# First phase of a two-layer diffusion backbone: quarter loads, modulation two chunks ahead, a fixed TensorE order, and later loads held back

## Chip, core and metric

The kernel runs on one core of a Trainium2 chip. The time is the device time of one execution in microseconds (us); the figure compared is the median of several executions. The kernel before took 1450.68 us (three runs, 1450.13 to 1450.79).

## What is computed

The reference runs two layers over 256 latent tokens and 256 context tokens of width 1024. Only the head of the first layer matters here:

```python
c_act = jax.nn.silu(c)
cc_act = jax.nn.silu(c_ctx)
...
mod = (c_act @ w_mod[i] + b_mod[i]).reshape(b, N_MOD, 1, d)
modc = (cc_act @ w_mod[i] + b_mod[i]).reshape(N_MOD, 1, d)
h = rms_norm(x, norm1_g[i]) * (1 + mod[:, 1]) + mod[:, 0]
hc = rms_norm(xc, norm1_g[i]) * (1 + modc[1]) + modc[0]
p = split_cols(h @ w_in[i])
pc = split_cols(hc @ w_in[i])
```

Six modulation vectors come from `w_mod`; the first two (scale and shift) must exist before the normalised input `h` can be formed, and `h` is needed by every projection in `w_in`. Four attention branches, a gated merge and a gated feed-forward network follow, then the second layer.

## The kernel before

**Tiling.** Everything is held transposed: the width 1024 is `KD` = 8 chunks of 128 partitions, the 512 tokens (256 latent, then 256 context) are the columns. Products are made in three parts: an operand is split into a rounded high half and the rest (`wh` and `wl` for weights, `hh` and `hl` for the input), and `mm3` (before, lines 278 to 280) multiplies high by high, high by low, low by high.

**The first phase.** It ends when the neighbourhood branch's keys and values (called keys below) are done. Its parts are:

- `xt`, the input, arrives in two loads; ScalarE squares its eight chunks, VectorE adds them into `ssf`. `rstd` (line 403 and on) sums over partitions on TensorE, takes the power -1/2 on GpSimd and spreads the result over partitions with TensorE again.
- `mods_chunk(c)`, for each chunk c: two 512-KB tiles of `w_mod` are loaded (`mraw`, line 370), sixteen products on TensorE give the scale and shift of chunk c (line 372), ScalarE copies them out of PSUM (`t`, line 375), two transposes turn them (line 378), VectorE reduces four parts into `M` (line 380).
- `modulate`: VectorE makes `t` from input, scale `s1` and `rstd`; ScalarE adds the shift and rounds, giving `hh` (line 424); VectorE forms the rest `hl`. This is done twice a chunk, for latent and for context tokens.
- `kv_mm`: twelve products of 512 columns a chunk, into three `acc` buffers and one `av` buffer of PSUM. The weights are four 512-KB tiles `raw` (line 264), two chunks each; ScalarE rounds a tile to `wh` (line 272), VectorE makes `wl` (line 257). Four buffers each exist for `raw`, `wh` and `wl`, and the next stages' weights use the same ones.

After the phase ScalarE copies values (`Vt`) and keys (`st`) out of PSUM, which frees an `acc` buffer for the query block `naq` (weights: two more tiles). The copy `dgt` (line 990) and the rope tables `rt` on GpSimd (line 257) need two 256-KB loads (lines 988 and 992). Between the attention stages `mods` computes the later modulation vectors on VectorE (`junk`, line 350, from a `raw` tile and `cact`, the activated conditioning spread over partitions).

**What sets the order.** Each engine runs its instructions in the order in which the build lists them. The build takes that order from a planner, which models when each instruction could start; the order in the source is only its input. All loads are issued by SyncE, one after the other, with eight in flight at most: a load waits until the eighth before it has landed, and for its buffer.

The names above and the lines that the change touches are in these functions:

## Time and profile before

| | |
|---|---|
| median of three runs | 1450.68 us |
| profiled execution | 1446.25 us, of which 1444.1 us span |
| TensorE busy | 1401.8 us (97% of the span) |
| VectorE, ScalarE, GpSimd busy | 1047.4, 657.8, 203.5 us |
| chain that ended last | TensorE 91%, VectorE 3%, ScalarE 2% |
| granted TensorE clock, mean | 0.994 of full speed |
| load traffic | 199.69 MB read, 139 GB/s over the span |

TensorE is busy nearly all the time, so a share of the whole span says little: what can move is where TensorE stands still, and most of that lies in the first 61 us. The views to read are the busy time by stretch for that part, and the timeline, whose bracket tells how long an engine stood before an instruction and what ended the wait.

### The profile page before, as it was taken

The numbers are of one execution on the slowest core, as the hardware profiler recorded it, in microseconds if no ns is written. First come the engines' busy times: TensorE is split into PE (matmuls) and PEld (weight loads), VectorE is DVE, ScalarE is ACT, GpSimd is POOL, SyncE is SP. The second block draws the span as 40 slices with busy tenths as digits, with TensorE's granted clock in tenths as the row PEclk, the third lists the DMA queues.
The fourth block names the chain that finished last, engine by engine and source line by source line (L and its number), as shares of the span: only waits on it lengthen the run. The fifth ranks groups of instructions, "written<-read, shape, count | busy, mean of one in ns | idle before, by whom it ended". The sixth has DMA issues, their size and how long they took to land.

```text
span 1444.1 us, 22450 instructions
## 1 busy us (share of the span) xinstructions
PE 1401.8 (97%) x8562; PEld 1191.2 (82%) x8562; DVE 1047.4 (73%) x1928; ACT 657.8 (46%) x1201; POOL 203.5 (14%) x191
## 2 busy tenths in 40 slices
PE   6899999999999999999999999999999999899999
PEld 3687778776777889888888888898888889799998
DVE  5588777657776557999999654767876676686884
ACT  5344554443333334543243432455655554564662
POOL 0242102223211200000000000053122411000000
PEclk9999999999999999999999999999999999899999
DMA  9432122223234441555797222232232334455553
GB/s 378 173 103 95 40 96 81 89 71 119 88 121 164 138 161 44 192 188 181 254 314 241 90 98 84 101 126 89 83 127 96 117 132 143 148 177 186 180 186 107
DMA packets 57931, 202.20 MB, mean 140 GB/s; under 512 B 6560, under 2 KB 8096, under 8 KB 57184
## 3 DMA queue, kind: packets, MB, share of 16 engines
q1 hardware_dynamic: 57824, 200.77, 40.4%
q8 instruction: 68, 1.11, 0.3%
q14 instruction: 39, 0.32, 0.1%
HBM read 199.69 MB, written 1.05 MB: 139 GB/s over the span
## 4 chain that ended last, share of the span: by engine, by line
PE 91%; DVE 3%; issue 2%; ACT 2%; POOL 1%; DMA 1%; SPq 0%; POOLq 0%; DVEq 0%; ACTq 0%
PE acc L278 26%; PE acc L279 26%; PE acc L280 25%; PE av L876 3%; PE sc L792 3%; PE tp L868 2%; DVE wl L257 1%; ACT wh L272 1%; PE tp L647 1%; PE sc L804 1%; PE acc L768 1%; DMA mraw<-in_wb_dram 1%; PE acc L728 1%; PE tp L372 0%; POOL st L257 0%
## 5 line engine op out<-in xcount | busy, mean ns | idle before, releaser
L272 ACT CAST wh<-raw 128x1024 fp32r<-128x1024 f32 (+1 forms) x272 | 279.7, 1029 | 457.3 <-PE acc L279 384.7
L257 DVE TENSOR_TENSOR wl<-raw,wh 128x1024 fp32r<-128x1024 f32 (+1 forms) x272 | 330.5, 1215 | 137.1 <-ACT wh L272 130.9
L278 PE MATMUL acc<-hh,wh 128*128 128x256 f32 (+1 forms) x1248 | 422.3, 340 | 5.7 <-ACT hh L424 3.9
L280 PE MATMUL acc<-hh,wl 128*128 128x256 f32 (+1 forms) x1248 | 417.6, 335 | 0.0
L279 PE MATMUL acc<-hl,wh 128*128 128x256 f32 (+1 forms) x1248 | 416.9, 335 | 0.0
L278 PEld LDWEIGHTS acc<-hh,wh 128*128 128x128 f32 x1248 | 237.8, 191 | 34.7 <-ACT hh L424 4.4
L279 PEld LDWEIGHTS acc<-hl,wh 128*128 128x128 f32 x1248 | 238.6, 191 | 24.3 <-issue 2.2
L280 PEld LDWEIGHTS acc<-hh,wl 128*128 128x128 f32 x1248 | 238.5, 191 | 23.7 <-issue 1.6
L350 DVE SCALAR_TENSOR_TENSOR junk<-raw,cact 128x1024 bf16<-128x1024 f32 x128 | 157.3, 1229 | 16.8 <-DMA raw<-in_wb_dram 16.1
L278 PE MATMUL acc<-wh,hh 128*128 128x256 f32 (+3 forms) x496 | 149.2, 301 | 5.9 <-ACT hh L424 5.8
L279 PE MATMUL acc<-wl,hh 128*128 128x256 f32 (+3 forms) x496 | 147.2, 297 | 0.0
L280 PE MATMUL acc<-wh,hl 128*128 128x256 f32 (+3 forms) x496 | 144.2, 296 | 1.0 <-DVE hl L254 1.0
L257 POOL TENSOR_TENSOR r<-v,mhalf 128x4 f32<-128x4 f32 (+3 forms) x59 | 79.5, 1352 | 431.0 <-DVE v L470 229.8
L279 PE MATMUL acc<-al,wh 128*128 128x256 f32 (+1 forms) x370 | 121.5, 328 | 0.0
L278 PE MATMUL acc<-ah,wh 128*128 128x256 f32 (+1 forms) x370 | 121.5, 328 | 0.0
L280 PE MATMUL acc<-ah,wl 128*128 128x256 f32 (+1 forms) x370 | 121.4, 328 | 0.0
L254 DVE SCALAR_TENSOR_TENSOR u<-acc,smt,u 128x255 f32<-128x255 f32 (+1 forms) x184 | 109.1, 595 | 1.2
L278 PEld LDWEIGHTS acc<-wh,hh 128*128 128x128 f32 x496 | 95.2, 192 | 15.0 <-ACT hh L424 8.3
L818 ACT ACTIVATE p<-sc,nm 128x512 f32<-128x512 f32 (+1 forms) x120 | 74.3, 620 | 70.7 <-DVE nm L815 37.0
L280 PEld LDWEIGHTS acc<-wh,hl 128*128 128x128 f32 x496 | 94.1, 191 | 8.3 <-issue 3.4
L279 PEld LDWEIGHTS acc<-wl,hh 128*128 128x128 f32 x496 | 95.3, 192 | 6.7 <-issue 4.2
L257 POOL TENSOR_TENSOR y<-y,t 128x512 f32<-128x512 f32 (+1 forms) x48 | 57.3, 1199 | 217.5 <-DVE t L254 185.2
(173 smaller groups left out, 2063.1 us busy)
## 6 DMA issues: line engine op xcount, KB each, us to landing
raw<-in_wb_dram SPq DMA_DIRECT2D x328, 512.0 KB, 3.4
mraw<-in_wb_dram SPq DMA_DIRECT2D x16, 512.0 KB, 10.2
raw<-in_wb_dram SPq DMA_DIRECT2D x20, 384.0 KB, 2.9
x<-in_xT_dram SPq DMA_DIRECT2D x2, 1024.0 KB, 6.1
bt<-in_bias_dram SPq DMA_DIRECT2D x8, 256.0 KB, 2.6
xt<-in_xT_dram SPq DMA_DIRECT2D x2, 1024.0 KB, 7.1
raw<-in_wb_dram SPq DMA_DIRECT2D x4, 320.0 KB, 2.8
cact<-in_cb_dram SPq DMA_DIRECT2D x1, 1024.0 KB, 11.4
```

Of the source, the lines that this page charges most:

```text
L254: return V.scalar_tensor_tensor(out=out, in0=in0, scalar=scalar, in1=in1, op0=op0, op1=op1)
L257: e.tensor_tensor(out=out, in0=a, in1=b, op=op)
L272: A.copy(h[:, :w], r[:, :w])
L278: mm(ps, lhsT=a[0], rhs=b[0], start=first, stop=False)
L279: mm(ps, lhsT=a[0], rhs=b[1], start=False, stop=False)
L280: mm(ps, lhsT=a[1], rhs=b[0], start=False, stop=last)
L350: V.scalar_tensor_tensor(out=junk, in0=r, scalar=1.0, in1=cact[:, st_], op0=ALU.mult, op1=ALU.mult, accum_out=o)
L647: nc.tensor.transpose(tp[:, g], got[0][:, g * P:(g + 1) * P], ident)
L792: mm(sps[:, :n], lhsT=q[o:o + d, c:c + P], rhs=k[o:o + d, T - n:], start=True, stop=True)
L818: A.activation(out=p[:, :n], in_=sps[:, :n], func=AF.Exp, bias=nm, accum_out=s)
L868: nc.tensor.transpose(tp[:, i], p[:, i * P:(i + 1) * P], ident)
L876: mm(av[64 * j:64 * j + 64], lhsT=V_[:, 4 - nk + i, vcol(hd):vcol(hd) + 64], rhs=PTs[j][:, i], start=i == 0, stop=i == nk - 1, tile_positi ...
```

## The change

It alters the first phase of layer 0 and the order of loads around it.

- The input comes in four loads of 512 KB rather than two of 1 MB. The small tables `smt` and the mask half of `C` move from the head of the load queue to behind the first modulation tiles and behind the last one.
- `mods_chunk` is cut in two: the products with the copy out of PSUM, and `mods_turn` (transposes and reduction). Loads, products and turns run two chunks ahead of the keys: in turn c the program issues the load and products of chunk c+2, the modulation and keys of chunk c, then the turn of chunk c+2.
- From the first modulation product to the last key product TensorE's instructions keep the order of the source (`manual_schedule`). The other engines' order stays with the planner.
- Every load made through `load` after the phase has the last modulation tile's load ahead of it in SyncE's queue (`hold`, `issue_after`). The load and activation of `cact` move behind the query block in the source.

```diff
+    hold = []
+    def load(out, in_):
+        with tc.issue_after(hold[0]) if hold else nullcontext():
+            nc.sync.dma_start(out=out, in_=in_)
...
+    def mods_load(c):
+        for hf in range(2):
+            m0[c, hf] = m0p.tile([P, 1024], F32, name="mraw")
+            m0["last"] = nc.sync.dma_start(out=m0[c, hf], in_=wb[0, KIDX["mod", 0, c, hf]])
...
     def mods_chunk(c):
...
-            r = m0p.tile([P, 1024], F32, name="mraw")
-            nc.sync.dma_start(out=r, in_=wb[0, KIDX["mod", 0, c, hf]])
+            r = m0[c, hf]
...
-        sb = tmp.tile([P, 512], F32, name="t")
+        sb = m0[c, "sb"] = tmp.tile([P, 512], F32, name="t")
         A.copy(sb[:, :256], ps[:, :256])
+
+    def mods_turn(c):
+        M, smt = Ms[0], smts[0]
+        sb = m0[c, "sb"]
         tp = tp_p.tile([P, 4, P], F32, name="tp")
...
-            small(0)
...
-            for h in range(2):
-                nc.sync.dma_start(out=xt[:, 4 * h:4 * h + 4], in_=xT[:, 4 * h:4 * h + 4])
+            for h in range(4):
+                nc.sync.dma_start(out=xt[:, 2 * h:2 * h + 2], in_=xT[:, 2 * h:2 * h + 2])
             nc.sync.dma_start(out=C[:, 0:256], in_=cst[:, 0:256])
+            mods_load(0)
+            small(0)
+            mods_load(1)
...
-            nc.sync.dma_start(out=C[:, 256:512], in_=cst[:, 256:512])
...
+            pes = ExitStack()
+            pes.enter_context(tc.manual_schedule(engines={nc.tensor.engine}))
             mods_chunk(0)
+            mods_chunk(1)
+            mods_turn(0)
             bcs = [rstd(accs, p_) for p_ in FULL]
+            mods_turn(1)
...
         for c in range(KD):
             if l == 0:
-                if c:
-                    mods_chunk(c)
+                if c % 2 == 0:
+                    w.append(wload(l, ("nakv", c // 2), 2, 512))
+                if c + 2 < KD:
+                    mods_load(c + 2)
+                    mods_chunk(c + 2)
...
             for t in range(4) if l == 0 else range(2):
                 kv_mm(c, t)
+            if l == 0 and c + 2 < KD:
+                mods_turn(c + 2)
+        if l == 0:
+            pes.close()
...
+        if l == 0:
+            hold.append(m0["last"].ins)
+            load(C[:, 256:512], cst[:, 256:512])
...
-            nc.sync.dma_start(out=cact, in_=cb)
-            A.activation(out=cact, in_=cact, func=AF.Silu)
...
         drive((first, 1))
+        if l == 0:
+            load(out=cact, in_=cb)
+            A.activation(out=cact, in_=cact, func=AF.Silu)
```

The lists below are each engine's instructions as built; a number behind a name tells one buffer use from another. Lines of the changed kernel are 7 to 46 higher than before.

**ScalarE around the first `hh`, before.** `raw_220` is the first weight tile of the keys, `t_212` and `t_216` are chunk 0.

```order
L375 COPY t_154<-tp_141 128x256
L272 CAST wh_222<-raw_220 128x1024
L424 ACTIVATE hh_101<-t_212,M_105 128x256
L375 COPY t_251<-tp_238 128x256
L272 CAST wh_312<-raw_310 128x1024
L424 ACTIVATE hh_101<-t_216,M_105 128x256
```

The same place with the change (`raw_235`, `325`, `415`, `505` are the four key tiles in their order, `t_257` and `t_261` chunk 0):

```order
L388 COPY t_172<-tp_163 128x256
L279 CAST wh_237<-raw_235 128x1024
L279 CAST wh_327<-raw_325 128x1024
L279 CAST wh_417<-raw_415 128x1024
L388 COPY t_254<-tp_245 128x256
L279 CAST wh_507<-raw_505 128x1024
L441 ACTIVATE hh_101<-t_257,M_121 128x256
L441 ACTIVATE hh_101<-t_261,M_121 128x256
```

One weight tile was rounded ahead of the first `hh`; now all four are.

**VectorE in the loop over chunks, before.** `red_256` and `t_260` belong to the same chunk, 1.

```order
L380 TENSOR_REDUCE red_256<-tp_253 128x4
L257 TENSOR_TENSOR M_105<-red_256,smt_103 128x2x2
L971 TENSOR_SCALAR s1_140<-M_105,smt_103 128x2
L254 SCALAR_TENSOR_TENSOR t_260<-x0_112,s1_140,sc_169 128x256
L254 SCALAR_TENSOR_TENSOR t_264<-x0_112,s1_140,sc_179 128x256
L254 SCALAR_TENSOR_TENSOR hl_102<-t_260,M_105,hh_101 128x256
```

With the change, at chunks 1 and 2 (`red_280` is the turn of chunk 2, `t_299` is chunk 1; `red_322` the turn of chunk 3, `t_347` chunk 2; `raw_625` is the first tile of `naq`):

```order
L397 TENSOR_REDUCE red_280<-tp_277 128x4
L257 TENSOR_TENSOR M_121<-red_280,smt_119 128x2x2
L997 TENSOR_SCALAR s1_149<-M_121,smt_119 128x2
L254 SCALAR_TENSOR_TENSOR t_299<-x0_109,s1_149,sc_187 128x256
...
L397 TENSOR_REDUCE red_322<-tp_319 128x4
...
L254 SCALAR_TENSOR_TENSOR t_347<-x0_109,s1_149,sc_187 128x256
L254 SCALAR_TENSOR_TENSOR t_351<-x0_109,s1_149,sc_197 128x256
L257 TENSOR_TENSOR wl_629<-raw_625,wh_627 128x1024
L254 SCALAR_TENSOR_TENSOR hl_102<-t_347,M_121,hh_101 128x256
```

The reduction ahead of a chunk's `t` is now that of the chunk after it, and the first `naq` tile stands between `t` and `hl` of chunk 2. On ScalarE the same stretch, from the copy of modulation chunk 4 to `hh` of chunk 4, now reads:

```order
L388 COPY t_344<-tp_335 128x256
L279 CAST wh_627<-raw_625 128x1024
L441 ACTIVATE hh_101<-t_347,M_121 128x256
L441 ACTIVATE hh_101<-t_351,M_121 128x256
L1046 ACT_TABLE_LOAD
L1046 ACTIVATE cact_99<-cact_99 128x2048
L388 COPY t_386<-tp_377 128x256
L557 ACT_TABLE_LOAD
L557 ACTIVATE le_8392<-ld_8390 128x2
L441 ACTIVATE hh_101<-t_389,M_121 128x256
...
L279 CAST wh_633<-raw_631 128x1024
L388 COPY t_434<-tp_425 128x256
L441 ACTIVATE hh_101<-t_437,M_121 128x256
```

**SyncE's loads behind the modulation tiles, before.** `raw_1020` to `raw_1239` are tiles of the differential branch, `t_551` and `t_555` the two rope loads.

```order
L264 DMA raw_1020<-in_wb_dram 128x1024
L832 DMA bt_824<-in_bias_dram 128x512
L264 DMA raw_1026<-in_wb_dram 128x1024
L264 DMA raw_1239<-in_wb_dram 128x1024
L988 DMA t_551<-in_rg_dram 128x512
L992 DMA t_555<-in_cst_dram 128x512
```

With the change, from the last modulation tile on (`raw_625`, `631`: `naq`; `790`, `796`, `1025`, `1031`, `1244`: differential branch; `951`: a later modulation tile; `t_556`, `t_560`: the rope loads):

```order
L376 DMA mraw_465<-in_wb_dram 128x1024
L267 DMA C_96<-in_cst_dram 128x256
L267 DMA raw_625<-in_wb_dram 128x1024
L267 DMA raw_631<-in_wb_dram 128x1024
L267 DMA cact_99<-in_cb_dram 128x2048
L267 DMA raw_790<-in_wb_dram 128x1024
...
L267 DMA raw_951<-in_wb_dram 128x1024
L267 DMA raw_1025<-in_wb_dram 128x1024
L267 DMA raw_1031<-in_wb_dram 128x1024
L267 DMA bt_829<-in_bias_dram 128x512
L267 DMA t_556<-in_rg_dram 128x512
L267 DMA raw_1244<-in_wb_dram 128x1024
L267 DMA t_560<-in_cst_dram 128x512
```

All of these now stand behind the last modulation tile; the two rope loads still stand behind `raw_1031` and `raw_1244`, which reuse the buffers of `raw_790` and `raw_796`.

## Rows read from the trace of the kernel before

**Rows 1.** Busy time by stretch (us, PE, PEld, DVE, ACT, POOL, PEclk, DMA share, GB/s).

```profile
15.00:20.00 5.00, 4.69 (x29) 3.34 (x30) 1.85 (x7) 0.13 (x1) 1.37 (x2) 1.00 1.03 410
...
45.00:50.00 5.00, 4.53 (x31) 2.59 (x30) 1.44 (x5) 1.00 (x2) 0.00 (x0) 1.00 0.14 57
...
55.00:60.00 5.00, 3.18 (x8) 2.48 (x8) 2.53 (x8) 1.15 (x3) 0.00 (x0) 0.67 0.60 210
```

**Rows 2.** Timeline (start us, length us, instruction, [wait before]): TensorE's start, first key product.

```profile
11.46 2.28 PE L372 MATMUL tp<-mraw,cs 128*32 128x256 f32 x16 [11.46 <-DMA mraw<-in_wb_dram]
...
12.66 0.20 PEld L372 LDWEIGHTS tp<-mraw,cs 128*32 128x32 f32 x8 [0.99 <-DMA mraw<-in_wb_dram]
...
20.93 0.79 PE L278 MATMUL acc<-wh,hh 128*128 128x512 f32 x1 [0.26 <-ACT hh L424]
```

**Rows 3.** Timeline, TensorE: a turn, a modulation chunk, two key products.

```profile
22.70 0.38 PE L378 MATMUL tp<-C,t 128*128 128x128 f32 x2
...
23.01 1.07 PE L372 MATMUL tp<-mraw,cs 128*32 128x256 f32 x16
...
24.58 0.39 PE L278 MATMUL acc<-wh,hh 128*128 128x512 f32 x1
...
24.81 0.40 PE L279 MATMUL acc<-wl,hh 128*128 128x512 f32 x1
```

**Rows 4.** Timeline, VectorE and ScalarE: one chunk's steps, one weight tile's steps.

```profile
21.04 1.05 ACT L272 CAST wh<-raw 128x1024 fp32r<-128x1024 f32 x1
...
22.11 1.23 DVE L257 TENSOR_TENSOR wl<-raw,wh 128x1024 fp32r<-128x1024 f32 x1 [0.53 <-ACT wh L272]
...
23.65 0.17 DVE L380 TENSOR_REDUCE red<-tp 128x4 f32<-128x16 f32 x1
...
24.32 0.87 DVE L254 SCALAR_TENSOR_TENSOR t<-x,s,sc 128x256 f32<-128x256 f32 x2
...
24.84 0.51 ACT L424 ACTIVATE hh<-t,M 128x256 fp32r<-128x256 f32 x1 [2.35 <-DVE t L254]
...
25.25 0.35 ACT L375 COPY t<-tp 128x256 f32<-128x256 f32 x1
...
25.38 0.48 DVE L254 SCALAR_TENSOR_TENSOR hl<-t,M,hh 128x256 fp32r<-128x256 f32 x1 [0.18 <-ACT hh L424]
...
27.91 1.28 ACT L1000 ACT_TABLE_LOAD   x1
```

**Rows 5.** Timeline, VectorE: a later modulation tile inside the phase.

```profile
51.21 1.22 DVE L350 SCALAR_TENSOR_TENSOR junk<-raw,cact 128x1024 bf16<-128x1024 f32 x1
```

**Rows 6.** Timeline, TensorE: two key products after a long wait.

```profile
57.51 0.63 PE L279 MATMUL acc<-wl,hh 128*128 128x512 f32 x1
57.93 0.63 PE L278 MATMUL acc<-wh,hh 128*128 128x512 f32 x1
```

**Rows 7.** Timeline: from the last keys to the query block.

```profile
59.36 0.24 ACT L990 COPY dgt<-t 128x64 f32<-128x64 f32 x1 [2.10 <-DMA t<-in_rg_dram]
...
60.76 0.37 ACT L661 COPY Vt<-acc 128x256 f32<-128x256 f32 x1 [1.16 <-PE acc L280]
61.03 0.38 ACT L669 COPY st<-acc 128x256 f32<-128x256 f32 x1
...
61.46 0.39 PE L278 MATMUL acc<-wh,hh 128*128 128x256 f32 x1
...
61.80 0.28 PE L280 MATMUL acc<-wh,hl 128*128 128x256 f32 x1
...
61.92 0.28 PE L278 MATMUL acc<-wh,hh 128*128 128x256 f32 x1
```

**Rows 8.** Timeline, GpSimd: rope tables, then three key scales.

```profile
60.33 2.82 POOL L257 TENSOR_TENSOR rt<-t 128x256 f32<-128x256 f32 x4 [6.77 <-DMA t<-in_cst_dram]
...
67.03 2.96 POOL L257 TENSOR_TENSOR r<-v,mhalf 128x4 f32<-128x4 f32 x3 [2.73 <-DVE v L470]
```

**Rows 9.** The page's load issues (count, KB each, median us from issue to landing).

```profile
raw<-in_wb_dram SPq DMA_DIRECT2D x328, 512.0 KB, 3.4
```

More of the change, by code (lines that the diff above doesn't have):

```diff
@@ L260, in lo_of @@
         tt(V, lo, full, hi.bitcast(F32), ALU.subtract)
+    hold = []
+    def load(out, in_):
+        with tc.issue_after(hold[0]) if hold else nullcontext():
+            nc.sync.dma_start(out=out, in_=in_)
     def wraw_load(l, key, n=1024):
         r = wraw.tile([P, 1024], F32, name="raw")
-        nc.sync.dma_start(out=r[:, :n], in_=wb[l, KIDX[key], :, :n])
+        load(r[:, :n], wb[l, KIDX[key], :, :n])
         return r
@@ L317, in small @@
         smts[l] = lay.tile([P, NSM], F32, name="smt")
-        nc.sync.dma_start(out=smts[l], in_=sm[l])
+        load(smts[l], sm[l])
         Ms[l] = lay.tile([P, 48, 2], F32, name="M")
@@ L333, in mods, with fetch @@
         got = []
-        def load():
+        def fetch():
             l, m, c = todo[len(got)]
@@ L338, in load @@
             g = [g for g in range(3) if m in MOD_GROUPS[g]][0]
-            nc.sync.dma_start(out=r, in_=wb[l, KIDX["mod", g, c, MOD_GROUPS[g].index(m)]])
+            load(r, wb[l, KIDX["mod", g, c, MOD_GROUPS[g].index(m)]])
             got.append(r)
@@ L343, in mods @@
             while len(got) < min(i + 1 + ahead, n):
-                load()
+                fetch()
             r, M = got[i], Ms[l]
@@ L362, in some @@
             yield
+    m0 = {}
+    def mods_load(c):
+        for hf in range(2):
+            m0[c, hf] = m0p.tile([P, 1024], F32, name="mraw")
+            m0["last"] = nc.sync.dma_start(out=m0[c, hf], in_=wb[0, KIDX["mod", 0, c, hf]])
     def mods_chunk(c):
@@ L705, in mla_weights @@
             mw["ka"], mw["qa"] = room[:, 1280:1536], room[:, 1536:2048].rearrange("p (k n) -> p k n", k=2)
-            nc.sync.dma_start(out=mw["kv"], in_=wb[l, KIDX["kvb",], :, :512])
-            nc.sync.dma_start(out=mw["q"][:96], in_=wb[l, KIDX["qb",], :96, :768].rearrange("p (k n) -> p k n", k=2))
+            load(out=mw["kv"], in_=wb[l, KIDX["kvb",], :, :512])
+            load(out=mw["q"][:96], in_=wb[l, KIDX["qb",], :96, :768].rearrange("p (k n) -> p k n", k=2))
         def use_mkv(t0, na, ps):
@@ L831, in probs_na @@
                     b = ptp.tile([P, 2, 256], F32, name="bt", bufs=1)
-                    nc.sync.dma_start(out=b, in_=bias[l, hd].rearrange("p (a k) -> p a k", a=2))
+                    load(out=b, in_=bias[l, hd].rearrange("p (a k) -> p a k", a=2))
                     tt(G, b, b, mask.unsqueeze(1).to_broadcast([P, 2, 256]), ALU.add)
@@ L975, in backbone @@
                     modulate(xt, bc, s1, M, 0, c, p_)
-            if c % 2 == 0:
+            if l and c % 2 == 0:
                 w.append(wload(l, ("nakv", c // 2), 2, 512))
@@ L984, in backbone @@
                     kv_mm(c, t)
+        if l == 0:
+            hold.append(m0["last"].ins)
+            load(C[:, 256:512], cst[:, 256:512])
         rt = lay.tile([P, 2, 2, 2, RW], F32, name="rt", bufs=1)
         rgt = tmp.tile([P, 4, RW], F32, name="t")
-        nc.sync.dma_start(out=rgt, in_=rg[l].rearrange("p (a w) -> p a w", a=4))
+        load(out=rgt, in_=rg[l].rearrange("p (a w) -> p a w", a=4))
         dgt = lay.tile([P, 2, 32], F32, name="dgt")
@@ L991, in backbone @@
         rtab0 = tmp.tile([P, 2, 2, RW], F32, name="t")
-        nc.sync.dma_start(out=rtab0, in_=cst[:, 512:].rearrange("p (a q w) -> p a q w", a=2, q=2))
+        load(out=rtab0, in_=cst[:, 512:].rearrange("p (a q w) -> p a q w", a=2, q=2))
         for j in range(2):
```

## Prediction

> **What bounds the kernel now.** I read the busy time by stretch first, then the timeline of the first 62 us on each engine. In the stretches the reader is to see two things. The load engines are full while the phase runs, at 410 GB/s, and nearly idle from 45 us on [rows 1]; yet TensorE is still at the keys until 61.46 us [rows 7], and the last of these stretches has it busy for 3.18 of 5 us at a mean clock of 0.67 [rows 1]. So loads set the beginning (TensorE's first product waits 11.46 us for a modulation tile, and the second tile is there at 12.66 us [rows 2]), and waits on VectorE and ScalarE set the end. After 61.46 us TensorE is the bound, 97% busy over the span, so what this phase wins or loses goes to the end nearly one for one. The phase is therefore the whole sum: when does the query block begin, 61.46 us before, and is TensorE held up behind it. All times below are from the span's start.
>
> **1. The first key product: 20.9 becomes 26.8 us.** Cutting the input into quarters and moving `smt` and half of `C` takes 319 KB from ahead of the second modulation tile: at 410 GB/s [rows 1] 0.8 us, so 12.66 becomes 11.9. That is a gain, but the first `hh` no longer hangs on it. ScalarE now rounds all four key tiles ahead of it, so the fourth must land. Behind the second modulation tile stand `smt` (191 KB), six more modulation tiles and four key tiles, 5311 KB or 5.44 MB: 13.3 us, hence 25.2. Rounding takes 1.05 and `hh` 0.51 [rows 4]: 26.8. Before it was 20.93 [rows 2], with one tile rounded ahead. The two chains of `rstd` now run one after the other, and modulation chunk 1 goes ahead of them; that hides under the same wait and costs nothing, as long as it ends by 26. The quarter loads are costed at nothing more for the same reason.
>
> Here the Trainium skill speaks against the change (DMA: Bandwidth & Descriptors, section Bandwidth): its rule is to batch transfers to 1 MiB or more, as smaller ones stay well under peak. The trace does not bear it out for this stream, which carries 410 GB/s with most of its loads at 512 KB [rows 1]. By the rule the input would come later; what that would make of the sum stands among the rivals.
>
> **2. TensorE's own work from there: 29.0 us.** 96 products at 0.23 apart (24.58 to 24.81), five modulation chunks at 1.0 (1.07 long, with its end overlapped), six turns at 0.31 [rows 3]: 22.1 + 5.0 + 1.9. Without a wait the keys would end at 55.8.
>
> **3. Waits between chunks: 10.6 us.** TensorE's order is now keys of c-1, turn of c+1, products of chunk c+2, keys of c. Call the end of the keys of c-1 zero: TensorE has passed the turn at 0.31 and is free at 1.3. If `hh` of chunk c were ready from the turn one round earlier, nothing would wait. But VectorE's list puts the reduction of the turn just done ahead of `t` of chunk c, so the lead of a round is lost. From the reduction to `t` is 0.67, to `hh` 1.19, to its end 1.7 [rows 4]; counted from 0.4 that is 2.1, so 0.85 of wait where nothing else stands in the list. What else does, chunk by chunk:
> - Chunk 0: VectorE makes the rests of the third and fourth key tiles ahead of `hl`, 1.23 each [rows 4]; the third product waits 0.3.
> - Chunk 1: the plain chain, 0.85.
> - Chunk 2: the copy of modulation chunk 4 (ready at 1.3, 0.35), then the rounding of the first `naq` tile (1.05), then `hh` (0.51): 3.3, which is 2.0 late. VectorE makes that tile's rest (1.23) ahead of `hl` (0.48), which adds 0.75: 2.75.
> - Chunk 3: the copy of chunk 5 (1.7), a table load of 1.28 [rows 4], the small exponential, `hh`: 3.8, so 2.5 late; and a `junk` of 1.22 [rows 5] ahead of `hl` adds 1.1: 3.6.
> - Chunk 4: rounding and rest of the second `naq` tile (2.4), then `t` and `hh`: 3.45, so 2.15.
> - Chunk 5: copy and `hh`: 1.0. Chunks 6 and 7 find theirs done.
>
> Two covers are thin. The last modulation tiles reuse buffers of chunk 3, whose products end near 33.5; the first `naq` tile, two loads and a small one behind, lands near 39, about when it is wanted. I count nothing, and up to 2 us in the range. The `cact` load, two further on, has some 3 us to spare. Sum: 66.4.
>
> **4. Low clock: 3.8 us.** After the last long wait TensorE's products stood 0.42 apart [rows 6] and not 0.23 [rows 3], with a mean granted clock of 0.67 in that stretch [rows 1]: 1.2 against 2.4 GHz. Ahead of the first key product TensorE stands again for some us, so I take its twelve products at 0.42 (2.3). The waits of chunks 2 to 4 are of the size that came before that fall [rows 1]; no row tells which of them will bring one. From below none, from above all 36 products (6.8); I take one fall of eight products (1.5), as in [rows 6]. Sum: 70.2.
>
> **5. The query block: 3.0 us.** It starts when ScalarE has emptied an `acc` buffer, behind the copy `dgt`, which waits for a rope load [rows 7]. Before, that load was there before the keys ended. Now it stands in SyncE's queue behind `raw_1031`, whose buffer comes free when VectorE has made the rest of `raw_790`, listed just ahead of `hl` of chunk 7. From the end of the keys of chunk 5: turn, reduction, both `t`, rest: 3.2; load 3.4 [rows 9]; two loads of 256 KB behind it at 0.64: 7.9; `dgt` 0.24, then 0.70 from `Vt` to the product [rows 7]: 8.85. TensorE is through with chunks 6 and 7 at 5.8. Sum: 73.2, against 61.46: **11.7 later**.
>
> **6. The rope tables: 4.0 us.** GpSimd's list has the tables `rt` (2.82 us) ahead of the second key scale (1.0 of 2.96) [rows 8]; TensorE turns those keys behind 68 products of the query block. Before, the tables began at 60.33, with the keys. Now their load is behind `raw_1244`, which waits for the rest of `raw_796`, whose rounding stands behind eight more copies and squares on ScalarE, 0.27 apart as `Vt` and `st` are [rows 7]. From the query block's start: 2.2 + 1.05 + 1.23, load 3.4 + 0.64, tables 2.82, scale 1.0: 12.5. TensorE gets there at 68 x 0.12 (61.80 to 61.92 [rows 7]) and two short turns, 8.5; a low clock in this block is inside the wait.
>
> Sum: 11.7 + 4.0 = 15.7 us. The profiled execution took 1446.25 us, 4.4 under the median of 1450.68; I carry the difference over to the median: **1466.4 us**. The planner also lists a few hundred rows behind this phase otherwise; up to 2 us either way, in the range.
>
> **Rivals.**
> - **The fixed order pays** (faster). The two-chunk lead and the loads that now come in order of need keep TensorE unbroken from 26.8: 55.8, the query block at once, 5.7 us gained: 1445.0. It decides itself at the chain of 1.7: it would have to fit beside a modulation chunk of 1.0, with the foreign tiles in gaps. For it: TensorE's own list needs nothing that is late by itself, and the modulation tiles land sooner. Against it: the lists of ScalarE and VectorE. 0.06.
> - **Only the plain chain bites** (no change). Naq tiles, table loads and `junk` find room, the clock holds, the rope loads come early: 55.8 + 0.3 + 5 x 0.85 = 60.4, 1449.6. 0.06.
> - **Waits without their echoes** (slower by half). The clock does not fall and the rope load costs no second wait: 26.8 + 29.0 + 10.6 + 3.0 = 69.4, that is +7.9: 1458.6. For it: the mean clock is 1.00 in most stretches [rows 1]. 0.13.
> - **Smaller loads are dearer.** A `raw` load lands 3.4 us after its issue [rows 9], of which 1.28 is its size at 410 GB/s; if two more input loads each exposed the other 2.1, everything in step 1 would come 4.2 later: 1470.6. Against it: eight loads are in flight. 0.04. This is how the Trainium skill's rule of step 1 would act.
>
> **How the numbers follow.** My forecast has 0.71. The range runs from just under the 1458.6 of the third rival to 1474: the clock low in all of chunks 2 to 4 (5.3 more) and the `naq` tile 2 us late. It leaves out the two fast cases and some 0.05 above. A change of 0.2%, 2.9 us, is about what can be told from none: faster 0.06, same 0.06, slower 0.88.
>
> **What would show it.** Right: the first key product near 27 us with `hh` behind the rounding of the fourth key tile; TensorE's waits before the keys of chunks 2, 3 and 4 of 2 to 4 us, ended by `hh` or `hl`; the query block near 73, with `dgt` ended by the rope load; one more wait on a transpose of keys some 8 us on. Load engines less than full between 30 and 45 us. Wrong: key products unbroken from 27 on, or a query block before 64; and if the first key product is there by 22, step 1 fails and with it half of the loss.

## The result, and the profile after

The changed kernel took 1463.15 us (median of five runs, 1462.6 to 1465.77) beside 1450.13 for the kernel before (five runs, 1447.59 to 1450.79): a ratio of 1.010, 95% interval 1.0083 to 1.0116, or 13.0 us slower. The forecast was 1466.4, with a range of 1457.5 to 1474.0.

The profiled execution took 1462.6 us, its span 1460.7. TensorE's timeline from its own chain to the query block (start, length, instruction, in brackets the wait before it and what ended it) answers to [rows 2]. From the first key product, at 28.35, on these are all the waits that the view marks; two pairs of rows show the pace of the products, and the turn (L395) behind each of chunks 0 to 3 shows where the chunk ended:

```profile
20.04 1.22 PE L426 MATMUL sc<-C,r 128*128 128x128 f32 x4 [2.04 <-POOL r L257]
...
22.94 1.22 PE L426 MATMUL sc<-C,r 128*128 128x128 f32 x4 [1.03 <-POOL r L257]
...
24.51 1.94 PE L385 MATMUL tp<-mraw,cs 128*32 128x256 f32 x16
28.35 0.80 PE L285 MATMUL acc<-wh,hh 128*128 128x512 f32 x1 [1.90 <-ACT hh L441]
...
29.89 0.80 PE L287 MATMUL acc<-wh,hl 128*128 128x512 f32 x1 [0.32 <-DVE hl L254]
...
30.91 0.63 PE L286 MATMUL acc<-wl,hh 128*128 128x512 f32 x1
31.34 0.63 PE L287 MATMUL acc<-wh,hl 128*128 128x512 f32 x1
...
32.87 0.40 PE L285 MATMUL av<-wh,hh 128*128 128x512 f32 x1
33.11 0.40 PE L286 MATMUL av<-wl,hh 128*128 128x512 f32 x1
...
33.57 0.38 PE L395 MATMUL tp<-C,t 128*128 128x128 f32 x2
...
35.85 0.50 PE L285 MATMUL acc<-wh,hh 128*128 128x512 f32 x1 [0.90 <-ACT hh L441]
...
38.78 0.38 PE L395 MATMUL tp<-C,t 128*128 128x128 f32 x2
...
43.43 0.80 PE L285 MATMUL acc<-wh,hh 128*128 128x512 f32 x1 [3.27 <-ACT hh L441]
...
49.11 0.63 PE L395 MATMUL tp<-C,t 128*128 128x128 f32 x2
...
53.16 0.79 PE L285 MATMUL acc<-wh,hh 128*128 128x512 f32 x1 [2.42 <-ACT hh L441]
54.55 0.80 PE L287 MATMUL acc<-wh,hl 128*128 128x512 f32 x1 [0.18 <-DVE hl L254]
...
57.88 0.38 PE L395 MATMUL tp<-C,t 128*128 128x128 f32 x2
...
61.37 0.50 PE L285 MATMUL acc<-wh,hh 128*128 128x512 f32 x1 [2.10 <-ACT hh L441]
...
66.58 0.50 PE L285 MATMUL acc<-wh,hh 128*128 128x512 f32 x1 [0.90 <-ACT hh L441]
...
73.36 0.50 PE L287 MATMUL acc<-wh,hl 128*128 128x512 f32 x1 [0.26 <-DVE hl L254]
...
75.76 0.28 PE L285 MATMUL acc<-wh,hh 128*128 128x256 f32 x1
```

The last row is the query block. It comes 14.3 us later than before (61.46 [rows 7]) and waits for nothing. The busy time by stretch (columns as in [rows 1]) shows the clock: low between 40 and 60 us, full again behind. The 1.00 of the first row below must be read with the products beside it: up to 32.6 us they stand 0.43 apart, as at the lower of the two levels (1.2 GHz, [rows 6]), and from 32.87 on 0.23 or 0.24, as at the higher (2.4 GHz). The trace's record of the granted clock begins only at 32.66 us, and the view counts time without a record as 1.00.

```profile
30.00:35.00 5.00, 4.95 (x28) 3.32 (x28) 1.17 (x6) 0.00 (x0) 0.00 (x0) 1.00 0.47 184
...
40.00:45.00 5.00, 1.71 (x7) 0.83 (x4) 2.61 (x5) 3.43 (x5) 0.00 (x0) 0.79 1.02 419
45.00:50.00 5.00, 5.00 (x20) 3.50 (x23) 0.21 (x3) 1.99 (x2) 0.00 (x0) 0.53 0.83 332
50.00:55.00 5.00, 2.40 (x19) 1.11 (x12) 3.90 (x15) 2.66 (x5) 0.00 (x0) 0.81 0.00 0
55.00:60.00 5.00, 4.27 (x28) 2.75 (x27) 2.45 (x6) 1.42 (x2) 0.00 (x0) 0.85 0.29 105
```

**A finer gauge.** Whole times of these kernels scatter by some 8 us from run to run, and a few short stretches of low clock come and go late in the program. For the phase itself I read the lag: how much later than in the kernel before (336.0 us from its span's start) the sixtieth softmax exponential on ScalarE begins, in the profiled executions. For the changed kernel it is 13.8 us, nearly all of the 14.3 at the query block; only 0.5 is given back in between.

### The profile page after: what moved, and what is told of

Read it like the earlier page. It is cut to its first block, busy times and chain, and to the rows that moved or that the text cites. A ratio compares the mean times of both kernels' runs of the same rounds, so it can differ in the third digit from the quotient of the medians.

```text
span 1460.7 us, 22445 instructions
## 1 busy us (share of the span) xinstructions
PE 1407.9 (96%) x8562; PEld 1195.5 (82%) x8562; DVE 1047.9 (72%) x1928; ACT 658.7 (45%) x1201; POOL 206.1 (14%) x191
## 3 DMA queue, kind: packets, MB, share of 16 engines
HBM read 199.69 MB, written 1.05 MB: 137 GB/s over the span
## 4 chain that ended last, share of the span: by engine, by line
PE 89%; DVE 3%; issue 2%; DMA 2%; ACT 2%; POOL 1%; POOLq 0%; SPq 0%; DVEq 0%; ACTq 0%
PE acc L285 26%; PE acc L287 25%; PE acc L286 25%; PE av L899 3%; PE sc L815 3%; PE tp L891 2%; DMA raw<-in_wb_dram 1%; DVE wl L257 1%; PE tp L670 1%; ACT wh L279 1%; PE sc L827 1%; DMA mraw<-in_wb_dram 1%; DVE t L254 1%; PE acc L791 1%; PE acc L751 1%
## 5 line engine op out<-in xcount | busy, mean ns | idle before, releaser
L287 PE MATMUL acc<-wh,hl 128*128 128x256 f32 (+3 forms) x496 | 148.6, 301 | 0.8 <-DVE hl L254 0.8
L841 ACT ACTIVATE p<-sc,nm 128x512 f32<-128x512 f32 (+1 forms) x120 | 74.2, 619 | 70.1 <-DVE nm L838 36.5
```

The source lines that it names most:

```text
L287: mm(ps, lhsT=a[1], rhs=b[0], start=False, stop=last)
L841: A.activation(out=p[:, :n], in_=sps[:, :n], func=AF.Exp, bias=nm, accum_out=s)
```

## Experiments

The question was what makes the loss. **T1**: the lists that the planner gives ScalarE and VectorE once TensorE's order is fixed. **R1**: TensorE's fixed order by itself. **R2**: the hold of the later loads. **R3**: the order and size of the first loads. All kernels compute the whole result. Work foreign to the phase is called foreign work below: rounding and rests of the `naq` tiles, `cact`'s table load and Silu, `junk`, the next layer's small exponential. Times of before differ a little from one set of runs to the next, so the ratios count.

| kernel | ratio to before (95%) | first key product | query block | lag |
|---|---|---|---|---|
| before | | 20.93 | 61.46 | 0 |
| the change | 1.0100 (1.0083 to 1.0116) | 28.35 | 75.76 | +13.8 |
| planner_pe | 0.9992 (0.9980 to 1.0004) | 25.08 | 60.93 | -0.5 |
| foreign_out | 1.0078 (1.0058 to 1.0098) | 28.96 | 70.13 | +10.2 |
| casts_later | 1.0093 (1.0072 to 1.0114) | 27.91 | 74.78 | +13.0 |
| no_hold | 1.0086 (1.0065 to 1.0106) | 28.32 | 70.57 | +8.7 |
| quarters | 1.0012 (0.9997 to 1.0028) | 21.88 | 61.98 | +0.8 |
| lead_foreign | 1.0092 (1.0074 to 1.0110) | 28.16 | 67.68 | +7.7 |
| lead_sums | 1.0041 (1.0024 to 1.0058) | 23.98 | 63.27 | +3.2 |
| foreign_in_gap | 1.0020 (1.0008 to 1.0033) | 24.03 | 63.26 | +1.6 |
| lists_cleared | 0.9935 (0.9920 to 0.9951) | 21.38 | 53.79 | -8.2 |
| cleared, planner_pe | 0.9984 (0.9973 to 0.9995) | 22.87 | 61.35 | -0.2 |
| cleared, no hold | 0.9952 (0.9936 to 0.9968) | 21.79 | 54.15 | -7.8 |

### planner_pe: TensorE's order back to the planner

```diff
-            pes.enter_context(tc.manual_schedule(engines={nc.tensor.engine}))
```

> The changed kernel in all else, but the block that fixes TensorE's order is left out, so the planner orders TensorE too. Its lists then come out otherwise: one key tile, not four, is rounded ahead of the first hh; the reduction of turn c+1 stands a round ahead of t of chunk c+1; the two naq tiles, the cact table and the small exponential stand only at chunks 6 and 7. Theory T1 (the loss comes from what the planner puts into ScalarE's and VectorE's lists when TensorE's order is fixed): first key product at 22 to 24 us, waits between chunks under 5 us in all, the low clock mostly gone, query block at 53 to 60 us, 1443 to 1451 us. Rival R2 (the later loads held behind the last modulation tile cost the time) and rival R3 (the new order of the first loads costs it): the loads are the changed kernel's, so the loss stays, 1458 us or more. Rival R1 (TensorE's fixed order costs by itself, whatever the other lists hold): as T1 here; the next two kernels part them.

1448.38 us against 1450.13, in T1's range. The loss is gone with the loads and the hold of the change in place, so R2 and R3 fall as its main cause. But T1's gain did not come: the first key product was late (25.08, not 22 to 24, as modulation chunk 3 stood ahead of it), the query block came at 60.93, no sooner than before, and the work that I expected at chunks 6 and 7 did stand there, in TensorE's way. A row of its timeline, and ScalarE's below it:

```profile
50.80 0.50 PE L285 MATMUL acc<-wh,hh 128*128 128x512 f32 x1 [3.18 <-ACT hh L441]
```

```profile
47.14 1.28 ACT L1045 ACT_TABLE_LOAD   x1
...
50.26 1.29 ACT L441 ACTIVATE hh<-t,M 128x256 fp32r<-128x256 f32 x3
```

### foreign_out: the foreign work behind the last chunk

```diff
+    def behind_keys(e):
+        return tc.issue_after(bar[e]) if e in bar else nullcontext()
...
-        A.copy(h[:, :w], r[:, :w])
+        with behind_keys("A"):
+            A.copy(h[:, :w], r[:, :w])
...
-        lo_of(lo[:, :w], r[:, :w], h[:, :w])
+        with behind_keys("V"):
+            lo_of(lo[:, :w], r[:, :w], h[:, :w])
...
+            bar.update(A=m0["A"].ins, V=m0["V"].ins)
```

(`m0["A"]` and `m0["V"]` are the last `hh` and `hl`; the same wrapper stands around `cact`'s Silu, `junk` and the small exponential's inputs.)

> TensorE's fixed order, the loads and the hold stay. Only the work that is foreign to the phase (rounding and rest of the naq tiles, the cact table and its Silu, the modulation sum called junk, the next layer's small exponential and its inputs) is queued behind the last hh on ScalarE and the last hl on VectorE. The four key tiles are still rounded ahead of the first hh. T1: first key product unchanged at 28.4 us; the waits before chunks 2, 3 and 4 fall from 3.27, 2.60 and 2.10 to 0.9 each; with .32, .90 and .90 that makes 4.8 in place of 10.35; the low clock falls from some 8 us to 2 to 4; query block at 64 to 67 us in place of 75.8, with up to 2 us given back where its first naq tile is now late. 1451 to 1456 us. R1: waits of the fixed order stay, 1459 us or more. R2 and R3: unchanged, 1461 to 1465 us.

1460.39 us, a miss: this is R1's range and not T1's, so the time does not part the two. Inside the phase it went as T1 said: the waits of 3.27, 2.60 and 2.10 are 0.90 each. But the query block came at 70.1, not 64 to 67, and the loss only fell from 13.8 to 10.2. TensorE's timeline:

```profile
28.96 0.50 PE L291 MATMUL acc<-wh,hh 128*128 128x512 f32 x1 [1.90 <-ACT hh L447]
...
57.59 0.50 PE L291 MATMUL acc<-wh,hh 128*128 128x512 f32 x1 [0.90 <-ACT hh L447]
...
70.13 0.39 PE L291 MATMUL acc<-wh,hh 128*128 128x256 f32 x1 [3.75 <-ACT st L702]
```

ScalarE's shows why: the work put off stands ahead of the first `Vt` and `st`, which free the buffer for the query block.

```profile
63.25 1.99 ACT L284 CAST wh<-raw 128x1024 fp32r<-128x1024 f32 x2
65.25 1.28 ACT L1058 ACT_TABLE_LOAD   x1
66.55 1.91 ACT L1058 ACTIVATE cact<-cact 128x2048 f32<-128x2048 f32 x1
...
69.44 0.36 ACT L694 COPY Vt<-acc 128x256 f32<-128x256 f32 x1
```

And some low clock stayed: 0.66 from 30 to 35 us, and 0.67 from 70 to 75. So foreign work is no waste to be pushed out; it must be done by then, and needs a place where its engine has room.

### casts_later: one key tile ahead of the first hh

```diff
+                    if c:
+                        with tc.issue_after(m0["A"].ins), tc.issue_after(m0["V"].ins):
+                            w.append(wload(l, ("nakv", c // 2), 2, 512))
```

> The changed kernel, but key tiles 2, 3 and 4 are rounded (and their rests made) behind the last hh and hl of the chunk before the one that they serve, so one tile stands ahead of the first hh. TensorE's order, loads and hold stay, and so does the foreign work. T1: TensorE has its own chain to 26.5 us (the two rstd chains one after the other, then modulation chunk 2), so the first key product only moves from 28.4 to 26.6 to 27; the waits behind it stay at 8 to 12 us. 1459 to 1463 us. If the four roundings were the main cause: 1452 us or less. R1, R2, R3: unchanged, 1461 to 1465 us.

1462.45 us, as expected. The first key product moved from 28.35 to 27.91, not to 26.6 to 27: it still hung on TensorE's own chain and then on the chain of `hh`. The four roundings ahead of it are therefore a small part of the loss as long as that chain stands.

### no_hold: the later loads not held

```diff
-            hold.append(m0["last"].ins)
```

> The changed kernel, but the later loads do not wait for the last modulation tile. By the lists four key tiles are still rounded ahead of the first hh; the cact table and Silu (1.28 and 1.91 us) and the small exponential's table (1.28) now stand between hh of chunks 0 and 1, the first naq tile between chunks 1 and 2, the second with junk at chunks 4 and 5. T1: the hold only decides where the foreign work falls, not how much of it there is: first key product at 28.4 us, the sum of the waits 8 to 13 us, 1458 to 1466 us. R2 (the held loads come late and this is the loss): back to 1450 to 1454 us, with the waits at chunks 2 and 3 gone.

1461.06 us. The waits before chunks 0 to 5 were 0.32 (third product), .95, 2.11, .91, 2.11 and .90: their sum, 7.3, is 3 below the change's, and under the 8 to 13 expected; behind them the clock was low only from 40 to 50 us (0.94 and 0.72). The lag is 8.7 in place of 13.8. So the hold has a share, through the lists: without it the first `naq` tile has landed when ScalarE wants it (with it, it lands at 41.9 and its rounding waits 1.32 for it, inside the 3.27). The expected 1458 to 1466 held, but some 4 us of its whole time come behind the sixtieth exponential. In the profiled executions that part took 1114.4 us, before 1108.1, at a mean granted clock of 0.990 and 0.994; the time at half clock there accounts for 4.2 of the 6.3 us, the rest stays open.

### quarters: the load order alone, on the kernel before

```diff
-            small(0)
...
-            for h in range(2):
-                nc.sync.dma_start(out=xt[:, 4 * h:4 * h + 4], in_=xT[:, 4 * h:4 * h + 4])
+            for h in range(4):
+                nc.sync.dma_start(out=xt[:, 2 * h:2 * h + 2], in_=xT[:, 2 * h:2 * h + 2])
             nc.sync.dma_start(out=C[:, 0:256], in_=cst[:, 0:256])
+            small(0)
```

> The kernel before in all else; only the input comes in four loads and the small table (smt) behind them and half of C, as in the change. R3 (the new order of the first loads costs the time): 1458 us or more. T1 (the lists of ScalarE and VectorE cost it): the second modulation tile is there some 0.5 to 0.8 us sooner and the rest stays, 1447 to 1451 us.

Within the measurement's reach of no change (ratio 1.0012, 0.9997 to 1.0028; lag 0.8). R3 falls as the cause of 13 us. The kernel leaves out that the change moves `smt` and half of `C` behind modulation tiles; planner_pe has these moves whole. The modulation tiles did not come sooner, as expected, but later: the first product, with the same bytes ahead of it, at 12.38, before at 11.46 [rows 2].

```profile
12.38 2.25 PE L372 MATMUL tp<-mraw,cs 128*32 128x256 f32 x16 [12.38 <-DMA mraw<-in_wb_dram]
```

The stretch of 5 to 10 us, in which the input lands, moved 375 GB/s, before 405; that of 10 to 15 us, with modulation tiles, 414 and 415.

### lead_foreign: VectorE and ScalarE in a fixed order too, a round ahead

```diff
-            pes.enter_context(tc.manual_schedule(engines={nc.tensor.engine}))
+            pes.enter_context(tc.manual_schedule(engines={nc.tensor.engine, nc.vector.engine, nc.scalar.engine}))
...
+                if c + 1 < KD:
+                    if c % 2:
+                        w.append(wload(l, ("nakv", (c + 1) // 2), 2, 512))
+                    scale_mod(c + 1)
                 if c + 2 < KD:
                     mods_load(c + 2)
                     mods_chunk(c + 2)
```

(`scale_mod` is `s1` and `modulate` of both halves; the foreign work is put off as in foreign_out.)

> TensorE's order is the changed kernel's, row for row; loads and hold too. On VectorE and ScalarE the order is fixed as well: scale, t, hh and hl of chunk c+1 ahead of the copy of modulation chunk c+2, so that each hh has a whole round of TensorE's work as its lead, and each key tile is rounded in the round before its first use. The foreign work stands behind the last hh and hl, as in the kernel foreign_out. T1: first key product at 26.5 to 27 us (TensorE's own chain), no wait of 0.9 at any chunk, keys end at 55.5 to 57; ScalarE begins the foreign work some 4 us sooner than in foreign_out (whose query block came at 70.1) and ends it near 57.5; query block at 56 to 59 us; 1444 to 1449 us. R1 (the fixed order of TensorE costs by itself): waits of the size of 0.9 remain, query block at 66 us or later, 1456 us or more.

1460.91 us, a miss (1444 to 1449 expected), and again in R1's range. The waits of 0.90 before `hh` were gone at every chunk, as T1 said, and three of 0.56 to 0.97 on the copy of a modulation chunk came in. But the first key product did not come sooner (28.16, TensorE waiting 2.74 for `hh`), and the query block waited 4.77 for ScalarE. Lag 7.7; the whole time has another 5 us behind the sixtieth exponential. In the profiled execution that part took 7.2 us more than before, 3.4 of them by a lower granted clock (0.991 for 0.994); the rest stays open.

### lead_sums: both column sums together

```diff
             mods_chunk(0)
+            rs = [rstd_sum(accs, p_) for p_ in FULL]
             mods_chunk(1)
             mods_turn(0)
-            bcs = [rstd(accs, p_) for p_ in FULL]
+            bcs = [rstd_bc(r) for r in rs]
             mods_turn(1)
```

> As the kernel lead_foreign, and in TensorE's fixed order the column sums of both halves stand behind modulation chunk 0, and the two rounds of spreading behind the turn of chunk 0, where the changed kernel has sum, spread, sum, spread with waits of 2.04 and 1.03 us for GpSimd between them. T1: those waits shrink to 0 to 1 us in all, the first key product comes at 23 to 24.5 us, some 3 us sooner than in lead_foreign; the keys end 3 us sooner, the query block only by 0 to 3, as it then waits for the foreign work on ScalarE (as in foreign_out, 3.75 us there). 1442 to 1447 us. R1: 1456 us or more.

1452.97 us, short of the 1442 to 1447 expected. The first key product (23.98, after a wait of 3.60 for `hh`) came 4.2 us sooner than in lead_foreign and the lag fell by 4.5: the serial chain of `rstd` is a part of the loss of its own, and the whole of it reached the end. The query block still waits for the foreign work:

```profile
63.27 0.58 PE L291 MATMUL acc<-wh,hh 128*128 128x256 f32 x1 [4.71 <-ACT st L721]
```

### foreign_in_gap: a first place for the foreign work

```diff
+                    if c + 2 == KD - 1:
+                        hold.append(m0["last"].ins)
+                        load(out=cact, in_=cb)
+                        A.activation(out=cact, in_=cact, func=AF.Silu)
                     mods_chunk(c + 2)
```

(Also: `dgt` and the next layer's small exponential behind the last `Vt`.)

> As the kernel lead_sums, but the foreign work is put where its engine has room: the cact load goes first behind the last modulation tile and its table and Silu (3.2 us) between hh of chunk 6 and the copy of modulation chunk 7; the copy dgt, which waits for a rope load, and the small exponential with its table go behind the last copy that empties a key buffer. T1: first key product at 23 to 24.5 us as in lead_sums, keys end at 52 to 54, query block within 1.5 us of that; 1439 to 1444 us, faster than the kernel before and than planner-ordered TensorE (1448.4). If the phase's end is bound by something else (the naq tiles' landing, the rope load), the query block stays at 56 us or later and the time at 1444 to 1449.

1451.29 us: better, and not the 1439 to 1444 expected. The place was wrong. ScalarE reached it only behind the `hh` of chunk 6, at 52.4 us, and the copy of modulation chunk 7 stood behind it, for which TensorE waited 3.79 us:

```profile
52.41 1.28 ACT L1039 ACT_TABLE_LOAD   x1
...
55.52 0.35 ACT L394 COPY t<-tp 128x256 f32<-128x256 f32 x1
```

### lists_cleared: the same TensorE order, lists set by hand

```diff
+            for bc, (a, b_, s) in zip(bcs, FULL):
+                hs.append(tmp.tile([P, T], F32, name="t")[:, :b_ - a])
+                stt(hs[-1], xt[:, c, a:b_], s1[:, c, s:s + 1], bc[:, :b_ - a], ALU.mult, ALU.mult)
...
+            for h_, b, (a, b_, s) in zip(hs, bs, FULL):
+                m0["A"] = A.activation(out=hh[:, c, a:b_], in_=h_, func=AF.Identity, bias=b)
...
                     mods_chunk(c + 2)
+                    if c + 2 == 6:
+                        nc.sync.dma_start(out=cact, in_=cb)
+                        A.activation(out=cact, in_=cact, func=AF.Silu)
...
+            bar.update(A=m0["A6"].ins, V=m0["V"].ins)
+            lambda_of()
```

> As the kernel foreign_in_gap, with what its trace showed amiss put right: the lambda of the first layer (a table load of 1.28, two small steps on VectorE and an exponential ahead of the rounding of the first key tile) goes behind the keys; within a chunk both t, then both hh, then both hl, in place of t, hh, hl by halves; t of chunk 0 ahead of the rest of the first key tile; each later key tile is rounded behind the hh of the chunk before; the cact load comes with the key loads and its Silu behind the copy of modulation chunk 6, not between hh of chunk 6 and the copy of chunk 7 (3.79 us of wait there); the naq tiles are rounded ahead of hh of chunk 7. TensorE's order is unchanged. T1: first key product at 21 to 22 us in place of 24.0, waits of TensorE from there to the query block under 2 us in all, keys end and query block at 51 to 54 us, that is 8 to 10 us sooner than before (61.46); the sixtieth softmax exponential 6 to 9 us sooner than in the kernel before; 1440 to 1444 us. R1 (the fixed order costs by itself): not sooner than foreign_in_gap, 1449 us or more.

1440.94 us (1437.84 to 1443.31): faster than the kernel before by 0.65% (interval 0.49 to 0.80%) and than the change by some 22 us. These are all of TensorE's waits from the first key product to the query block, at full clock throughout:

```profile
21.38 0.50 PE L291 MATMUL acc<-wh,hh 128*128 128x512 f32 x1 [0.64 <-ACT hh L1028]
...
22.37 0.50 PE L292 MATMUL acc<-wl,hh 128*128 128x512 f32 x1 [0.48 <-DVE wl L257]
...
31.82 0.64 PE L391 MATMUL tp<-mraw,cs 128*32 128x256 f32 x8 [1.52 <-DMA mraw<-in_wb_dram]
...
39.77 1.07 PE L391 MATMUL tp<-mraw,cs 128*32 128x256 f32 x16
...
43.93 1.07 PE L391 MATMUL tp<-mraw,cs 128*32 128x256 f32 x16
...
53.79 0.28 PE L291 MATMUL acc<-wh,hh 128*128 128x256 f32 x1
```

```profile
50.00:55.00 5.00, 5.00 (x29) 4.16 (x28) 4.81 (x10) 4.12 (x14) 0.79 (x1) 1.00 0.69 209
```

TensorE's list in this phase has the order of the change but for the two sums. R1 falls: with these lists the fixed order costs nothing.

### The same lists, TensorE free; the same lists, no hold

```diff
-            pes.enter_context(tc.manual_schedule(engines={nc.tensor.engine, nc.vector.engine, nc.scalar.engine}))
+            pes.enter_context(tc.manual_schedule(engines={nc.vector.engine, nc.scalar.engine}))
```

> As the kernel lists_cleared, with the lists of ScalarE and VectorE fixed as there, but TensorE's order left to the planner. This prices TensorE's fixed order by itself, with nothing else moved in the two lists of that phase. T1 (the lists cost, the order does not): within 3 us of lists_cleared on either side, 1438 to 1444 us. R1 (the fixed order costs): faster than lists_cleared by over 3 us, 1437 us or less. If the fixed order is what gains here: 1445 us or more.

1447.34 us, a ratio of 0.9984. That is neither T1's 1438 to 1444 nor R1's 1437: beside these lists the fixed order gains. ScalarE's list in the phase is the same, row for row, and the query block is 7.6 us later than in lists_cleared: the planner lets TensorE begin a chunk whose weight tile that list has not yet rounded. Three such waits make 5.0 of the 7.6 (the third, of 1.46, is at 54.52):

```profile
31.99 0.96 PE L291 MATMUL acc<-wh,hh 128*128 128x512 f32 x3 [1.46 <-ACT wh L284]
...
42.86 0.97 PE L291 MATMUL acc<-wh,hh 128*128 128x512 f32 x3 [2.12 <-ACT wh L284]
```

Orders belong together. TensorE fixed and the others not: 1.010. The others fixed and TensorE not: 0.9984. None fixed: 0.9992. All three: 0.9935. (The first and the third have the source order of the change, the other two that of lists_cleared.)

```diff
-            hold.append(m0["last"].ins)
```

> As the kernel lists_cleared, but without the hold; the lists of ScalarE and VectorE up to the query block are the same rows. SyncE then has the second half of C and the next layer's small table (320 KB, 0.8 us at 410 GB/s) ahead of the modulation tiles of chunk 4, and the first naq tile ahead of those of chunk 7. T1: TensorE's wait for the tile of chunk 4 (1.52 us in lists_cleared) grows by 0.8; all else stays; 1440 to 1443 us. R2 (held loads come late and cost time): faster than lists_cleared by 3 us or more.

1443.07 us, lag -7.8 in place of -8.2: with the lists set by hand the hold is worth 0.4 us or nothing (the intervals of the ratios overlap). R2 falls here. The wait for the tiles of chunk 4 did not grow by 0.8: it came to 0.38 and 1.05, for 1.52.

## Why the prediction was right, step by step

The sign and the size were right (13.0 us measured, 15.7 forecast), by the mechanism forecast: waits on `hh` and `hl` that the lists of ScalarE and VectorE set, and low clock behind them. Single steps were off in both directions, and that the total came within 2.7 us is in part luck. Of the signs named in advance the late first key product and the waits of 2 to 4 us before chunks 2 to 4 came; the rope load ahead of the query block and a later wait on a transpose did not.

- **Step 1, first key product 26.8: 28.35.** Mis-sized by 1.55. I said that the two chains of `rstd` one after the other would hide "as long as it ends by 26". It ended at 26.45 (24.51 + 1.94, modulation chunk 2), after waits of 2.04 and 1.03 for GpSimd, and the copy of chunk 2 stands ahead of the fourth rounding in ScalarE's list, which the step left out. ScalarE's timeline:

```profile
26.57 0.37 ACT L388 COPY t<-tp 128x256 f32<-128x256 f32 x1 [1.23 <-PE tp L385]
26.84 1.05 ACT L279 CAST wh<-raw 128x1024 fp32r<-128x1024 f32 x1
27.79 0.91 ACT L441 ACTIVATE hh<-t,M 128x256 fp32r<-128x256 f32 x2
```

  casts_later and lead_sums show which of the two mattered: without the extra roundings 0.4 us came back, with the sums together (lead_foreign to lead_sums) 4.2.
- **Step 2, own work 29.0: 30.4.** In lists_cleared, 53.79 - 21.38 less the two waits is 30.4, at full clock. A modulation chunk and a turn take 1.4, not 1.31: rounds start 4.16 apart (39.77 to 43.93), less twelve products at 0.23.
- **Step 3, waits 10.6: 10.35.** By chunk .32, .90, 3.27, 2.60, 2.10, .90, 0, .26 against .3, .85, 2.75, 3.6, 2.15, 1.0, 0, 0. The parts come out as in the lists: the lost lead of a round is the 0.90 (0.85 in the step, whose own terms give 0.8; foreign_out has it at every chunk from 1 to 5, lead_foreign at none), the rest is foreign work. At chunk 2 `hh` was 1.27 later than forecast, as its rounding waited 1.32 for the `naq` tile, the thin cover that I named. The waits on `hl` hardly showed (chunk 2 none marked for 0.75, chunk 3 0.18 for 1.1): `hl` did stand behind the tile's rest and behind `junk` (52.81 to 53.96), but the two products ahead of it went at the lower clock and covered it.
- **Step 4, low clock 3.8: 6.6.** Mis-sized by 2.8, the step that was furthest short. Chunk 1's twelve products, at full clock, took 2.93 (35.85 to 38.78). Chunk 0's took 4.90 without their wait (28.35 to 33.57), 2.0 more, where I had 2.3. Chunk 2's took 5.68 (43.43 to 49.11), 2.75 more, some 0.2 of it for `hl`, and the turn behind them 0.25 more; chunk 3's 4.54 without their wait (53.16 to 57.88), 1.6 more. So there were two falls behind the first products, and the first lasted a whole chunk, where I took one fall of eight products (1.5); the 6.8 that I named as the upper bound is nearly what came. The parts close: 30.4, 10.35 and 6.6 are the 47.4 from 28.35 to 75.76.
- **Steps 5 and 6, 3.0 and 4.0: both 0.** Wrong. (Step 6's terms add up to 12.3, not 12.5.) They rest on a statement made ahead of the prediction, that `raw_1031` and `raw_1244` reuse the buffers of `raw_790` and `raw_796`. The trace shows each a tile sooner: `raw_1031`, the third load in the first row below, went out at 60.41, right behind the rest of `raw_631` (59.16 + 1.23), and `raw_1244` at 72.94, behind that of `raw_790` (71.69 + 1.22), since `raw_1025` took the buffer that `raw_951` had given back in between. SyncE's timeline:

```profile
44.25 16.49 SPq L267 DMA_DIRECT2D raw<-in_wb_dram  x3
...
69.95 0.33 SPq L267 DMA_DIRECT2D t<-in_rg_dram  x1
72.94 0.33 SPq L267 DMA_DIRECT2D raw<-in_wb_dram  x1
```

  The rope load of 69.95 waited not for `raw_1031` but for the turn of modulation chunk 7 (its wait of 3.8 ended with it), which reads a `t` tile, and the load takes a `t` buffer. `dgt` followed at 72.52 after a wait of 0.19, ahead of the end of the keys; the rope tables began at 77.00 and TensorE waited for neither.

The overrun of steps 1, 2 and 4, less that of step 3 (1.55 + 1.4 + 2.8 - 0.25 = 5.5), nearly pays for the 7.0 of steps 5 and 6, so the time came out better than its parts. The rival "waits without their echoes" was right that the rope loads give no second wait, and wrong on the clock. "The fixed order pays" was wrong for the planner's lists, and lists_cleared shows it right for lists set by hand. "Smaller loads are dearer" was too dear at 4.2 us: quarters shows up to 0.9, one execution against one, and the start of the first modulation product scatters by 0.7 (11.04 to 11.72) among the eleven kernels with the change's load order. The Trainium skill's rule to batch transfers to 1 MiB or more (DMA: Bandwidth & Descriptors, section Bandwidth) agrees with the stretch of 5 to 10 us, where the twelve kernels with quarters moved 348 to 383 GB/s and the kernel before 405. It does not show in the stream behind, of 512-KB loads, at 414 and 415 GB/s.

## What to carry to other kernels

When you fix one engine's order under a planner, read the lists that it then gives the other engines: what the fixed engine waits for is set there, and here work foreign to the phase landed ahead of the very step that was waited for. Fix the engines of a loop together, give each product's inputs a whole round of lead, and find foreign work a place where its engine has room, neither in the chain nor all at its end. Before you trust a buffer's turn in a pool, derive it from who gives one back first, not from counting.

## What the runs showed of the hardware

- **The granted clock of a stretch needs the products beside it.** In the change the record of the clock begins at 32.66 us, in the kernel before at 22.56; ahead of that the products stand 0.43 apart, the pace of the lower level, though the stretches read 1.00.
- **The clock does not follow the size of a wait alone.** Behind the same waits ahead of the first key product (2.04, 1.03, 1.90) TensorE began the keys at the lower level in the change and at the higher in foreign_out, where the products stood 0.43 apart only from 30.94 on (0.66 from 30 to 35 us). In no_hold two waits of 2.11 had different ends: behind the first the clock fell, behind the second it did not. In lead_sums it fell to 0.66 behind a single 3.60; in lists_cleared no wait above 1.52 followed the first key product, and no stretch up to 75 us was below 1.00. The rows of no_hold:

```profile
42.99 0.50 PE L285 MATMUL acc<-wh,hh 128*128 128x512 f32 x1 [2.11 <-ACT hh L441]
...
56.16 0.50 PE L285 MATMUL acc<-wh,hh 128*128 128x512 f32 x1 [2.11 <-ACT hh L441]
```

```profile
45.00:50.00 5.00, 4.09 (x25) 2.43 (x24) 1.61 (x6) 1.08 (x3) 0.00 (x0) 0.72 0.02 9
...
55.00:60.00 5.00, 3.84 (x26) 2.80 (x30) 2.28 (x8) 0.91 (x2) 0.00 (x0) 1.00 0.49 164
```

- **A table load goes when functions are sorted.** In lists_cleared the Silu of `cact` has no table load ahead of it, because the first layer's exponential moved behind it; in the change that load took 1.28 us, and the small exponential's another 1.28. The Trainium skill's rule to batch activations by table set (ScalarE: Activation LUTs, section Table sets: the hidden batching unit) agrees: up to 60 us ScalarE has four such loads in the change and two in lists_cleared. What that gained of the whole time was not measured apart. The Silu in lists_cleared:

```profile
42.17 1.92 ACT L1047 ACTIVATE cact<-cact 128x2048 f32<-128x2048 f32 x1
```
